# A diffusion step on one core: the weight sums for the way down spread evenly, and the last half product divided at column 320

## The chip, the cores and the metric

The kernel runs on one core of a Trainium2 chip, as one launch. The metric is the device time of an execution in microseconds (us), a median over runs. Five engines work side by side: TensorE (PE, matmuls, with PEld its weight loads), VectorE (DVE), ScalarE (ACT), GpSimd (POOL), and SyncE (SP), which issues nearly all DMA transfers. Each engine takes its instructions strictly in the order of its own queue; a waiting instruction holds what stands behind it.

## The reference

The model is one layer of a diffusion backbone: a half-step FFN, a token mixer (attention and a recurrent scan), a second half-step FFN, and a last RMSNorm. The change lies in the second FFN and the last norm:

```python
x = x + 0.5 * m[8] * swiglu(modulate(x, norm_g[2], m[6], m[7]), *ffn2)   # end of the layer
def swiglu(h, w1, w3, w2):
    return (jax.nn.silu(h @ w1) * (h @ w3)) @ w2
def rmsnorm(x, g):
    xf = x.astype(jnp.float32)
    xf = xf * lax.rsqrt(jnp.mean(xf * xf, axis=-1, keepdims=True) + EPS)
    return (xf * g.astype(jnp.float32)).astype(x.dtype)
```

x has 1152 tokens (1024 latent and 128 context) and D = 1024 features; w1 and w3 are 1024 x 2816, w2 is 2816 x 1024, all in float32. Modulation and gates differ between latent and context tokens.

## The kernel before, in words

**Layout.** Features lie on the 128 partitions, tokens along the free axis: T = 1152 columns, HALF = 576, quarters of QW = 288. The hidden features make NF = 22 blocks `f` of 128. A float32 product is made of three matmuls on parts in the reduced type fp32r: high by high, high by low, low by high. So each matrix needs a high part (a cast on ACT) and a low part (a subtraction on DVE).

**The way up, `ffn_fast(1, ...)`.** Blocks 0 to 2 are plain (`plain_block`). Blocks 3 to 21 are done by a Strassen-Winograd scheme: `fast_block` runs seven products, in the order `PRODUCTS = (1, 6, 7, 5, 2, 4, 3)`, in place of eight. For each product two blocks of tokens (r = 0, 1) take 12 matmuls each of 128 x 288 (L1865), so 24 matmuls are one product, and 19 x 7 = 133 products follow one another. Evictions on ACT and DVE (L1867 to L1883) turn the sums into SiLU(...) times (...), and SP stores the result to `hs` in DRAM (L1757).

The weights of each product are made by the generator `fast_ops`: SP loads two halves of `raw` for each f (L1818, two buffers), POOL adds and subtracts quarters of the weight matrix in pieces of 256 columns (L1836), ACT casts the high part (L1840), DVE subtracts it for the low part (L1841). The list `made` holds the weights of six products ahead of the one in work; their tiles are six buffers under two tags.

**The weight sums for the way down, `combos(w2)`.** The way down also uses seven products instead of eight, so it needs sums of quarters of w2. `combos` makes them in 22 sets (11 blocks `kk` by two halves `v` of the columns). For one set SP loads four pieces of 128 x 256 (L591), POOL makes four additions (L594, L595, L597, L598), and SP stores four results to `wc` in DRAM (L601). The pieces lie in three buffers of one tag and one of another, so a set's loads need the buffers that the last set's stores set free. The generator is advanced once a product (`next(wsum, None)`); a set has five `yield`s, so 22 sets are 110 steps.

**What sets the order.** A scheduler orders the instructions on each engine by costs and due times, not simply in the order in which the program was written, unless an instruction goes through `keep_in_program_order`; that ties it behind the instruction written before it on its engine, without a semaphore. The sums do not go through it before the change.

**The way down, `way_down`.** Six products of the scheme are swept in 66 steps (six products of HF = 11 steps each, 8 cells x 3 matmuls of 128 x 288 per step, L731). SP loads the hidden features `h` (L618) and weights `raw` (L636), DVE and ACT prepare the parts. `gated` adds a finished sum to x (L578). The generator is already advanced from the second product of the last f on, so its first loads stand beside the last products of the way up.

**The last half product and the end.** The last product concerns only half of the tokens (columns 0 to HALF) and four of the eight feature blocks. It is divided at column CUT: first `b0`, columns 0 to CUT, with the first HEAD = 7 of the 11 steps taken step by step over four banks (m = 0 to 3), then the remaining four for one m after the other; then `b1`, columns CUT to HALF, m by m. Its right-hand sides come from `prep3(j)` (L672 cast, L673 subtraction) and its weights from `cast_w3`. Beside it stands the RMSNorm: `square` and the sums over m on POOL (L694, L818), `root` (a matmul by ones called `nps`, L702, then ACT L406 and L407 and DVE L408 to L410), and `finish`, which scales x (DVE L499; ACT L496 and POOL L497 for some m) and issues the stores of the output (L500). The right half of the tokens, `root(HALF, T)` and `finish(HALF, T)`, is dealt with inside `b0`; `root(0, CUT)` is called in the middle of the first m of `b1`, after 18 of its 33 matmuls; `root(CUT, HALF)` and the last `finish` close the program.

Of the kernel before, what the change touches and what calls it, by code (L numbers as in the profile page):

```python
# [9 lines left out]
F32 = mybir.dt.float32  # L10
# [10 lines left out]
P = 128  # L21
# [26 lines left out]
HALF = 2 * QW  # L48
HF = NF // 2
SWEEP = (2, 1, 6, 7, 4, 5)  # L50
STEPS = len(SWEEP) * HF
CELLS = (0, 0, "st"), (1, 0, "up"), (2, 0, "up"), (0, 1, "ps1"), (1, 1, "dn"), (2, 1, "dn"), (3, 0, "up"), (3, 1, "dn")
CUT = 384
HEAD = 7


# [41 lines left out]
class Trunk:  # L98
# [480 lines left out]

    def combos(self, w2):  # L580

        nc = self.nc
        self.wc = self.dp.tile([4, HF, P, HALF - 64], F32, name="wc")
        n = 256
        for kk in range(HF):
            for v in range(2):
                lo, hi = slice(v * n, v * n + n), slice(512 + v * n, 512 + v * n + n)
                t = [self.fp.tile([P, QW], F32, tag="hf", bufs=3, name="wc")[:, :n] for _ in range(3)]
                a11, a21, a22, a12 = t + [self.slim("wc")[:, :n]]
                for o, f, c in ((a22, kk + HF, hi), (a21, kk, hi), (a11, kk, lo), (a12, kk + HF, lo)):  # L590
                    nc.sync.dma_start(o, w2[f][:, 0, c])  # L591
                yield
                yield
                nc.gpsimd.tensor_add(a22, a22, a21)  # L594
                nc.gpsimd.tensor_sub(a21, a11, a21)  # L595
                yield
                nc.gpsimd.tensor_sub(a11, a22, a11)  # L597
                nc.gpsimd.tensor_sub(a12, a12, a11)  # L598
                yield
                for i, o in enumerate((a22, a21, a11, a12)):  # L600
                    nc.sync.dma_start(self.wc[i, kk][:, lo], o)  # L601
                yield

    def way_down(self, w2, gm):

        nc = self.nc
# [7 lines left out]
        def load(g, j, h):  # L614
            if kt[g][j] is None:
                new = partial(self.tt, F32) if not g or j < 3 else self.wide
                kt[g][j] = new(name=f"h{g}")
            nc.sync.dma_start(kt[g][j][:, half[h]], self.hs[g * HF + j][:, half[h]])  # L618

        def load_x(m, cs):  # L620
            if self.x[m] is None:
                self.x[m] = self.tt(F32, f"x{m}")
            nc.sync.dma_start(self.x[m][:, cs], self.xs[m][:, cs])
# [9 lines left out]
        def load_w(p):  # L633
            t = raws[p] = self.wp.tile([P, 2, 512], F32, tag="raw", bufs=2, name="raw")
            for v in range(2):
                nc.sync.dma_start(t[:, v], src(2 * p + v))  # L636

        def cast_w(p):
            t = raws.pop(p)
            wh = self.wp.tile([P, 2, 512], F32R, tag="wh", bufs=3, name="wh")  # L640
            wl = self.wp.tile([P, 2, 512], F32R, tag="wl", bufs=3, name="wl")
            nc.scalar.copy(wh, t)  # L642
            nc.vector.tensor_sub(wl, t, wh)  # L643
            for v in range(2):
                W[2 * p + v] = wh[:, v], wl[:, v]

        def first(j):
            t = kt[0][j]
            nc.vector.tensor_sub(t[:, B], t[:, B], t[:, A])  # L649

        def second(j):
            t = kt[1][j]
            nc.vector.tensor_sub(t[:, B], t[:, B], kt[0][j][:, B])  # L653

        def prep(s):
            i, j = SWEEP[s // HF], s % HF
            h0, h1 = kt[0][j], kt[1][j]
            if i == 7:
                nc.vector.tensor_sub(h0[:, A], h1[:, B], h0[:, A])
            elif i == 4:  # L660
                nc.vector.tensor_sub(h1[:, A], h1[:, A], h1[:, B])
            v = {2: (h1, A), 1: (h0, A), 6: (h1, B), 7: (h0, A), 4: (h1, A), 5: (h0, B)}[i]
            v = v[0][:, v[1]]
            hi, lo = self.half("xh", F32R), self.half("xl", F32R)
            nc.scalar.copy(hi, v)
            nc.vector.tensor_sub(lo, v, hi)  # L666
            X[s] = hi, lo

        def prep3(j):
            t = kt[1][j]  # L670
            hi, lo = F(t[:, A]), F(t[:, B])
            nc.scalar.copy(hi, t[:, B])  # L672
            nc.vector.tensor_sub(lo, t[:, B], hi)  # L673

        def load_w3(j):
            t = self.tt(F32, "w3")
            nc.sync.dma_start(t[:, 512:1024], self.wc[3, j])
            w3.append(t)

        def cast_w3(j):  # L680
            t = w3[j]
            nc.scalar.copy(F(t[:, :512]), t[:, 512:1024])
            nc.vector.tensor_sub(F(t[:, 512:1024]), t[:, 512:1024], F(t[:, :512]))

        def square(m, lo, hi):
            acc = self.rs[:, lo:hi]
            if m == (0 if lo else 4):
                nc.scalar.activation(acc, self.x[m][:, lo:hi], AF.Square)
                return
            for c in range(lo, hi, QW):  # L690
                sq = self.slim("sq")
                n = min(QW, hi - c)
                nc.scalar.activation(sq[:, :n], self.x[m][:, c : c + n], AF.Square)
                nc.gpsimd.tensor_add(self.rs[:, c : c + n], self.rs[:, c : c + n], sq[:, :n])  # L694
# [40 lines left out]
        def taken(i, m, r):  # L735
            a, b = HALF + r * QW, r * QW
            outs = {2: ((0, a),), 1: ((0, a),), 6: ((0, b),), 7: ((4, b),), 4: ((4, a),), 5: ((4, b), (0, b))}
            for o, lo in outs[i]:
                self.gated(m + o, banks[m, r], lo, lo + QW, gm)

        for s in range(STEPS):
            i, kk = SWEEP[s // HF], s % HF
            if s % 2 == 0 and s // 2 + 1 < STEPS // 2:
                cast_w(s // 2 + 1)
                if s // 2 + 2 < STEPS // 2:
                    load_w(s // 2 + 2)
            if s + 6 < HF:
                load(1, s + 6, "a")
            if s in (1, 3, 5, 7):
                load_x(s // 2, A)  # L750
            for g, h, at in ((0, "a", 4), (0, "b", 9), (1, "b", 14), (1, "b", 44)):
                if at <= s < at + HF:
                    if at == 44:
                        kt[1][s - at] = None
                    load(g, s - at, h)
            if 25 <= s < 29:
                load_x(s - 25, B)
            if s in (30, 32, 34, 36):
                load_x(s // 2 - 11, slice(0, T))
            if 14 <= s < 14 + HF:  # L760
                first(s - 14)
            if 20 <= s < 20 + HF:
                second(s - 20)
            if s == 45:
                self.lnexp()
            if s == 50:
                self.new_rs()
            if 52 <= s < 52 + HF:
                load_w3(s - 52)
            if 54 <= s < 54 + HF:  # L770
                cast_w3(s - 54)
            if s + 2 < STEPS:
                prep(s + 2)
            if s > 56 and s % 2:
                prep3((s - 57) // 2)
            if 57 <= s < 57 + KT:
                square(s - 57, HALF, T)
            if kk == 0 and i in (2, 1, 5):
                banks = {(m, r): self.bank(tag, "down") for m, r, tag in CELLS}
            if s == STEPS - 2:  # L780
                continue
            both = s == STEPS - 1
            cells = sorted(CELLS, key=lambda c: c[1]) if both else CELLS
            for m, r, _ in cells:
                if both:
                    mms(s - 1, m, r, False, False)
                mms(s, m, r, kk == 0 and i not in (6, 7, 4), kk == HF - 1)
                if kk == HF - 1:
                    taken(i, m, r)

        b0 = [self.bank(t, "down", CUT) for t in ("st", "up", "up", "up")]

# [3 lines left out]
            self.mm3(ps, [(wh, wl, xh, xl)], start=j == 0, stop=j == HF - 1)  # L796

        for j in range(HEAD):
            if j + 5 < HF:
                prep3(j + 5)  # L800
            for m in range(4):
                mm(b0[m], m, j, 0, CUT)
            if j == 2:
                for r in range(2):
                    root(HALF + r * QW, HALF + (r + 1) * QW, ("dn", "ps1")[r])
            if j == 3:
                self.finish(HALF, T)
            if j > 2:
                square(j + 1, 0, HALF)
        b1 = [self.bank(t, "down", HALF - CUT) for t in ("dn", "dn", "dn", "ps1")]  # L810
        for m in range(4):
            for j in range(HEAD, HF):
                mm(b0[m], m, j, 0, CUT)
            self.gated(m, b0[m], 0, CUT, gm)
            sq = self.half("sq")[:, :CUT]
            nc.scalar.activation(sq, self.x[m][:, :CUT], AF.Square)
# [1305 lines left out]
```

## Time and profile before

| what | number |
|---|---|
| median of 3 runs | 2995.68 us (2993.05 to 2998.06) |
| profiled execution | 2989.97 us, its span 2988.2 us |
| mean granted clock of TensorE | 0.981 |
| stage of the fast blocks, second FFN | about 2248 to 2724 us of the span |
| the sums (first load to last store) | about 2172 to 2446 us |
| the sweep of the way down | to 2937.6 us |
| the last half product and the end | 2937.6 to 2988.2 us |

The profiled execution is 5.7 us below the median, so a sum is made against the execution's own 2989.97 us. A row of a window gives the stretch, then busy time and number of instructions for each engine asked for, the granted clock (1.00 is full), the share of the DMA engines and what they moved. A row of groups gives line, engine, operation, tiles and shapes, then busy time and mean duration in ns, then the idle time ahead of it and what ended it. A row of waits gives who waited for whom, the total, how often, and the longest.

### The profile page before, as it was taken

The page shows a single profiled execution, that of the slowest core. Times are in us where ns is not written, and L with a number is a line of the kernel's source. Part 1 is how long each engine was busy: PE and PEld are TensorE (multiplying, and loading weights), DVE is VectorE, ACT ScalarE, POOL GpSimd, SP SyncE. Part 2 cuts the span into 40 slices and gives each one's busy share as a digit, 9 for nine tenths or more (in the row PEclk, how much of TensorE's full clock was granted, in tenths as well). Part 3 has the DMA queues.
Part 4 walks back from the last instruction along what each step waited for, and adds up shares of the span by engine and source line. Part 5 has one row for each costly group of instructions (what it writes and reads, how often), then busy time and mean ns, then how long its engine had stood idle before and what let it go on. Part 6 is the DMA issues. An engine that isn't in the chain of part 4 may idle for free. (4 is left out here: it accounts for less than half of the span.)

```text
span 2988.2 us, 57736 instructions
## 1 busy us (share of the span) xinstructions
PE 2852.0 (95%) x22928; PEld 2711.9 (91%) x22928; DVE 1903.2 (64%) x3655; ACT 1179.4 (39%) x2218; POOL 1040.3 (35%) x967
## 2 busy tenths in 40 slices
PE   7999999999989999999998999899999789999998
PEld 5999999999988989898996777699999779999998
DVE  7787777566657657575247776856664445556865
ACT  5432322221273435342236777721542222323453
POOL 3233323553143333332244444533345542220003
PEclk9999999999999999999998999999999889999999
DMA  6643343632111111111201111342445652227442
GB/s 236 203 144 122 121 128 111 227 115 68 54 61 62 39 54 39 55 39 59 77 13 36 41 32 59 100 158 82 163 156 163 197 165 73 75 76 262 154 140 78
DMA packets 187214, 316.61 MB, mean 106 GB/s; under 512 B 23168, under 2 KB 110272, under 8 KB 186944
## 3 DMA queue, kind: packets, MB, share of 16 engines
q1 hardware_dynamic: 186800, 312.83, 32.0%
q8 instruction: 180, 2.95, 0.4%
q14 instruction: 90, 0.74, 0.1%
q10 hardware_dynamic: 144, 0.10, 0.0%
HBM read 237.79 MB, written 75.06 MB: 105 GB/s over the span
## 5 line engine op out<-in xcount | busy, mean ns | idle before, releaser
L1865 PE MATMUL b<-xo,wo 128*128 128x288 f32 x3552 | 491.0, 298 | 17.6 <-DVE et L1871 17.6
L1865 PEld LDWEIGHTS b<-xo,wo 128*128 128x128 f32 x3552 | 481.6, 190 | 18.6 <-DVE et L1871 18.6
L1865 PE MATMUL b<-bh,wo 128*128 128x288 f32 x1776 | 372.4, 299 | 20.1 <-ACT et L1875 20.1
L506 PE MATMUL mm<-xh,wh 128*128 128x384 f32 (+1 forms) x1008 | 354.2, 351 | 26.4 <-DVE sg L939 13.8
L508 PE MATMUL mm<-xh,wl 128*128 128x384 f32 (+1 forms) x1008 | 343.5, 341 | 0.8 <-DVE wl L246 0.8
L507 PE MATMUL mm<-xl,wh 128*128 128x384 f32 (+1 forms) x1008 | 343.2, 340 | 0.7 <-issue 0.7
L246 POOL TENSOR_TENSOR wl<-raw,wh 128x1024 fp32r<-128x1024 f32 (+1 forms) x92 | 206.3, 2244 | 369.6 <-ACT wh L245 338.5
L1865 PEld LDWEIGHTS b<-bh,wo 128*128 128x128 f32 x1776 | 294.9, 192 | 20.9 <-ACT et L1875 20.9
L535 DVE SCALAR_TENSOR_TENSOR x<-dn,modt,x 128x384 f32<-128x384 f32 (+4 forms) x440 | 211.3, 499 | 119.6 <-PE dn L508 118.7
L1865 PE MATMUL b<-bl,wo 128*128 128x288 f32 x888 | 264.9, 298 | 0.0
L506 PEld LDWEIGHTS mm<-xh,wh 128*128 128x128 f32 (+1 forms) x1008 | 190.8, 189 | 35.5 <-DVE sg L939 15.5
L1841 DVE TENSOR_TENSOR wo<-raw,wo 128x512 fp32r<-128x512 f32 x185 | 129.8, 703 | 132.9 <-ACT wo L1840 130.9
L1840 ACT CAST wo<-raw 128x512 fp32r<-128x512 f32 x185 | 114.1, 621 | 232.7 <-PE b L1865 100.3
L507 PEld LDWEIGHTS mm<-xl,wh 128*128 128x128 f32 (+1 forms) x1008 | 191.2, 190 | 3.5 <-issue 2.2
L508 PEld LDWEIGHTS mm<-xh,wl 128*128 128x128 f32 (+1 forms) x1008 | 191.0, 189 | 2.1 <-DVE wl L246 1.1
L1597 POOL TENSOR_TENSOR ehl<-e,ehl 128x512 fp32r<-128x512 f32 x93 | 122.9, 1322 | 144.8 <-ACT ehl L1595 65.1
L1865 PEld LDWEIGHTS b<-bl,wo 128*128 128x128 f32 x888 | 170.8, 192 | 0.0
L245 ACT CAST wh<-raw 128x1024 fp32r<-128x1024 f32 (+3 forms) x97 | 92.8, 959 | 163.8 <-PE mm L507 61.5
L731 PE MATMUL down<-xh,wh 128*128 128x288 f32 x528 | 156.4, 297 | 0.5 <-DVE x L578 0.5
L731 PE MATMUL down<-xl,wh 128*128 128x288 f32 x528 | 155.9, 296 | 0.8 <-DVE xl L666 0.8
L731 PE MATMUL down<-xh,wl 128*128 128x288 f32 x528 | 156.1, 296 | 0.0
L1836 POOL TENSOR_TENSOR ws<-raw 128x256 f32<-128x256 f32 x74 | 67.7, 934 | 250.7 <-DMA raw<-in_w 227.2
(419 smaller groups left out, 7284.7 us busy)
## 6 DMA issues: line engine op xcount, KB each, us to landing
raw<-in_w SPq DMA_DIRECT2D x181, 256.0 KB, 3.1
hs<-et SPq DMA_DIRECT2D x148, 144.0 KB, 1.8
raw<-in_w_in SPq DMA_DIRECT2D x41, 512.0 KB, 3.7
wada<-in_w_aT SPq DMA_DIRECT2D x80, 256.0 KB, 2.9
raw<-in_w SPq DMA_DIRECT2D x36, 512.0 KB, 3.7
wada<-in_w_ada SPq DMA_DIRECT2D x32, 512.0 KB, 4.0
h<-hs SPq DMA_DIRECT2D x55, 288.0 KB, 5.1
hb<-hd SPq DMA_DIRECT2D x44, 288.0 KB, 3.6
```

The costliest lines, as they stand in the source:

```text
L245: pin(self.nc.scalar.copy(wh, raw))
L246: pin((eng or self.nc.gpsimd).tensor_sub(wl, raw, wh))
L506: nc.tensor.matmul(ps, wh, xh, start=start and i == 0, stop=False)
L507: nc.tensor.matmul(ps, wh, xl, start=False, stop=False)
L508: nc.tensor.matmul(ps, wl, xh, start=False, stop=stop and i == n - 1)
L535: nc.vector.scalar_tensor_tensor(self.x[m][:, a:b], ps[:, a - lo : b - lo], self.modt[:, gm, m, s : s + 1], self.x[m][:, a:b], ALU.mult, A ...
L731: nc.tensor.matmul(banks[m, r], w, x, start=first and i == 0, stop=last and i == 2, skip_group_check=chain)
L1597: eng.tensor_sub(el, e, eh)
L1836: nc.gpsimd.tensor_tensor(o[:, c], x[:, c], y[:, c], op)
L1840: nc.scalar.copy(wh, src[i])
L1841: nc.vector.tensor_sub(wl, src[i], wh)
L1865: nc.tensor.matmul(ps, w[:, k], x[:, k, :QW], start=first, stop=last, skip_group_check=home != i)
```

## The change

It has three parts. First, `combos`: a set now has six `yield`s (a step between the last additions and the stores), so 22 sets are 132 steps, and each load, addition and store goes through `keep_in_program_order`. (The DRAM tile is written as 512 columns where HALF - 64 stood, which is the same number.) Second, CUT becomes 320: the left part of the last half product is 320 columns wide instead of 384, the right part 256 instead of 192; and inside the left part `root(HALF, T)` and `finish(HALF, T)` are called after six steps (j == 5) instead of after three and four, and the squares of x for m = 4 to 7 at j = 0 to 3 instead of 3 to 6. Third, `prep3` is called at steps 48 to 63 of the sweep, in the fifth and sixth product, instead of at odd steps from 57 on and in the first steps of the left part.

```diff
-CUT = 384
+CUT = 320
...
-        nc = self.nc
-        self.wc = self.dp.tile([4, HF, P, HALF - 64], F32, name="wc")
+        nc, pin = self.nc, self.tc.keep_in_program_order
+        self.wc = self.dp.tile([4, HF, P, 512], F32, name="wc")
...
                 for o, f, c in ((a22, kk + HF, hi), (a21, kk, hi), (a11, kk, lo), (a12, kk + HF, lo)):
-                    nc.sync.dma_start(o, w2[f][:, 0, c])
+                    pin(nc.sync.dma_start(o, w2[f][:, 0, c]))
                 yield
                 yield
-                nc.gpsimd.tensor_add(a22, a22, a21)
-                nc.gpsimd.tensor_sub(a21, a11, a21)
+                pin(nc.gpsimd.tensor_add(a22, a22, a21))
+                pin(nc.gpsimd.tensor_sub(a21, a11, a21))
                 yield
-                nc.gpsimd.tensor_sub(a11, a22, a11)
-                nc.gpsimd.tensor_sub(a12, a12, a11)
+                pin(nc.gpsimd.tensor_sub(a11, a22, a11))
+                pin(nc.gpsimd.tensor_sub(a12, a12, a11))
+                yield
                 yield
                 for i, o in enumerate((a22, a21, a11, a12)):
-                    nc.sync.dma_start(self.wc[i, kk][:, lo], o)
+                    pin(nc.sync.dma_start(self.wc[i, kk][:, lo], o))
                 yield
...
+        third = [48 + (3 * j + 1) // 2 for j in range(HF)]
...
-            if s > 56 and s % 2:
-                prep3((s - 57) // 2)
+            if s in third:
+                prep3(third.index(s))
...
         for j in range(HEAD):
-            if j + 5 < HF:
-                prep3(j + 5)
             for m in range(4):
                 mm(b0[m], m, j, 0, CUT)
-            if j == 2:
+            if j == 5:
                 for r in range(2):
                     root(HALF + r * QW, HALF + (r + 1) * QW, ("dn", "ps1")[r])
-            if j == 3:
                 self.finish(HALF, T)
-            if j > 2:
-                square(j + 1, 0, HALF)
+            if j < 4:
+                square(j + 4, 0, HALF)
```

What this does to the order of the instructions is best seen at three places. Line numbers of the changed kernel are one higher between its lines 602 and 741, and one lower behind its line 831; L1835 there is L1836 before, L602 is L601.

The first place is POOL in the middle of the fast blocks. L1836 makes the pre-additions of the products' weights (`ws`, `raw`); the other rows are additions of sets. Before:

```order
L1836 TENSOR_TENSOR raw<-raw,ws 128x256 x2
L594 TENSOR_TENSOR wc<-wc 128x256
L595 TENSOR_TENSOR wc<-wc 128x256
L597 TENSOR_TENSOR wc<-wc 128x256
L598 TENSOR_TENSOR wc<-wc 128x256
L594 TENSOR_TENSOR wc<-wc 128x256
L595 TENSOR_TENSOR wc<-wc 128x256
L597 TENSOR_TENSOR wc<-wc 128x256
L598 TENSOR_TENSOR wc<-wc 128x256
L1836 TENSOR_TENSOR ws<-raw 128x256 x2
```

And now:

```order
L1835 TENSOR_TENSOR raw<-raw,ws 128x256 x2
L1835 TENSOR_TENSOR ws<-raw 128x256 x2
L1835 TENSOR_TENSOR ws<-ws,raw 128x256 x2
L1835 TENSOR_TENSOR raw<-raw 128x256 x2
L594 TENSOR_TENSOR wc<-wc 128x256
L595 TENSOR_TENSOR wc<-wc 128x256
L597 TENSOR_TENSOR wc<-wc 128x256
L598 TENSOR_TENSOR wc<-wc 128x256
L1835 TENSOR_TENSOR raw<-raw,ws 128x256 x2
```

Two whole sets stood in a gap between pre-additions, up to four in one f, and behind the middle of the stage none were left. Now about one set stands in each f, up to the last.

The second place is SP at the change from the way up to the way down. `hs` are stores of the way up, `h` and `raw` of L636/L637 loads of the way down. Before:

```order
L1818 DMA raw<-in_w 128x512 x2
L636 DMA raw<-in_w 128x512 x2
L1757 DMA hs_23744<-et 128x288 x4
L618 DMA h_29454<-hs_23744 128x576
L618 DMA h_29456<-hs_23744 128x576
L618 DMA h_29489<-hs_23744 128x576
L636 DMA raw<-in_w 128x512 x2
L618 DMA h_29538<-hs_23744 128x576
```

And now:

```order
L637 DMA raw<-in_w 128x512 x2
L1756 DMA hs_23744<-et 128x288 x2
L602 DMA wc<-wc 128x256 x4
L1756 DMA hs_23744<-et 128x288 x2
L591 DMA wc<-in_w 128x256 x4
L619 DMA h_29446<-hs_23744 128x576
L619 DMA h_29448<-hs_23744 128x576
L619 DMA h_29483<-hs_23744 128x576
L637 DMA raw<-in_w 128x512 x2
L619 DMA h_29534<-hs_23744 128x576
L619 DMA h_29562<-hs_23744 128x576
L602 DMA wc<-wc 128x256 x4
```

The last set's loads and stores (`wc`) now stand among the first loads of the way down, where none stood.

The third place is DVE in the last half product: L578 adds a finished sum to x, L408 to L410 are the end of a `root`, L499 belongs to `finish`. Before, from the last L499 over the right half of the tokens on:

```order
L499 SCALAR_TENSOR_TENSOR x_30924<-x_30924,vec,rs 128x576
L578 SCALAR_TENSOR_TENSOR x_29683<-down,modt,x_29683 128x384
L578 SCALAR_TENSOR_TENSOR x_29752<-down,modt,x_29752 128x384
L578 SCALAR_TENSOR_TENSOR x_29821<-down,modt,x_29821 128x384
L578 SCALAR_TENSOR_TENSOR x_29890<-down,modt,x_29890 128x384
L408 SCALAR_TENSOR_TENSOR rt<-nps,rs 128x384
L409 SCALAR_TENSOR_TENSOR rt<-rt,rs 128x384
L410 SCALAR_TENSOR_TENSOR rs<-rt,rs 128x384
```

And now:

```order
L499 SCALAR_TENSOR_TENSOR x_30924<-x_30924,vec,rs 128x576
L578 SCALAR_TENSOR_TENSOR x_29683<-down,modt,x_29683 128x320
L578 SCALAR_TENSOR_TENSOR x_29752<-down,modt,x_29752 128x320
L578 SCALAR_TENSOR_TENSOR x_29821<-down,modt,x_29821 128x320
L578 SCALAR_TENSOR_TENSOR x_29890<-down,modt,x_29890 128x320
L408 SCALAR_TENSOR_TENSOR rt<-nps,rs 128x320
L409 SCALAR_TENSOR_TENSOR rt<-rt,rs 128x320
L578 SCALAR_TENSOR_TENSOR x_29683<-down,modt,x_29683 128x256
```

The six L499 over the right half still stand ahead of the four evictions of the left part, though their `root` is now called three steps later on PE; the widths change, and the first eviction of the right part moves ahead of the last root operation.

## The prediction

> **What bounds the kernel now.** I read the page first, for the share of each engine and the chain of waits.
>
> ```profile
> span 2988.2 us, 57736 instructions
> PE 2852.0 (95%) x22928; PEld 2711.9 (91%) x22928; DVE 1903.2 (64%) x3655; ACT 1179.4 (39%) x2218; POOL 1040.3 (35%) x967
> PE b L1865 9%; PE down L731 6%; PE down L508 0%; PE down L507 0%; PE down L506 0%; DMA h<-hs 0%; DVE wl L643 0%; POOL rs L694 0%; PE nps L702 0%; DVE xl L666 0%; DVE h L649 0%; DMA raw<-in_w 0%; ACT wh L642 0%; DVE x L499 0%; DVE h L653 0%
> ```
>
> TensorE (PE) is busy for 95%, and the chain runs over two matmul lines: L1865, the products of the fast blocks, and L731, the way down. A saving must close a gap in PE, make a matmul cheaper, or shorten what follows the last one. So the next view is windows over L1865 alone: three stretches of the second FFN, and the same code in the first FFN, which makes no weight sums.
>
> ```profile
> core 0: us, PE busy (x) PEld busy (x), PEclk, DMA share, GB/s
> 2248.60:2288.60 40.00, 39.97 (x300) 39.80 (x300) 1.00 0.51 161
> 2288.60:2450.70 162.10, 125.64 (x854) 124.28 (x853) 0.89 0.58 186
> 2450.70:2724.00 273.30, 273.27 (x2040) 273.03 (x2040) 0.99 0.28 93
> 154.00:557.00 403.00, 401.71 (x3023) 401.52 (x3024) 1.00 0.40 129
> ```
>
> In the first FFN 3024 matmuls take 403 us, 133.3 ns each. In the second FFN 40 us run at that pace, then 162.1 us hold 854 matmuls, which at 133.3 ns need 113.8 us, and the last 273 us are full again. The loss of the stage is 162.1 - 113.8 = **48.3 us**, all in one stretch. The waits of PE from 2240 to 2724 us and two rows of its timeline say what it consists of.
>
> ```profile
> PE b L1865 <- ACT et L1875: 18.8, 3, 7.6
> PE b L1865 <- DVE et L1871: 17.6, 4, 6.3
> 2352.96 3.15 PE L1865 MATMUL b<-xo,wo 128*128 128x288 f32 x12 [3.63 <-DVE et L1871]
> 2438.09 4.99 PE L1865 MATMUL b<-xo,wo 128*128 128x288 f32 x24 [2.50 <-DVE et L1871]
> ```
>
> Seven stalls make 36.4 us. The other 12 us are slow matmuls behind them: 12 take 3.15 us where the pace gives 1.6, and 24 take 4.99 instead of 3.2. The named releasers (L1871, L1875) are the last evictions ahead; they cannot be the cause, since the first FFN runs them too. All waits of the same stretch show the cause:
>
> ```profile
> ACT wo L1840 <- POOL ws L1836: 78.7, 6, 16.4
> POOL wc L594 <- DMA wc<-in_w: 39.7, 11, 5.0
> ACT wo L1840 <- POOL raw L1836: 30.7, 10, 10.2
> SPq L601 <- POOL wc L594: 35.9, 16, 5.7
> ```
>
> The cast L1840, which makes the next weights, waits 109 us for GpSimd's (POOL's) pre-additions L1836, and POOL stands 39.7 us at L594 for the loads of a set of weight sums. Its order explains it: two whole sets stand in one gap between pre-additions, and the second set's loads need buffers that the first set's stores must free, so POOL waits in order with the products' additions behind it.
>
> **The change part by part. Sums spread out.** The POOL groups of this stretch, and the last two rows the stretch after it, in which no sums are left:
>
> ```profile
> L595 POOL TENSOR_TENSOR wc<-wc 128x256 f32<-128x256 f32 x17 | 15.5, 913 | 3.3 <-issue 1.5 <-POOL wc L594 0.4 <-DMA wc<-in_w 0.2
> L597 POOL TENSOR_TENSOR wc<-wc 128x256 f32<-128x256 f32 x17 | 15.2, 891 | 1.3
> L598 POOL TENSOR_TENSOR wc<-wc 128x256 f32<-128x256 f32 x17 | 14.2, 836 | 1.3
> L594 POOL TENSOR_TENSOR wc<-wc 128x256 f32<-128x256 f32 x17 | 14.0, 826 | 52.3 <-DMA wc<-in_w 39.7 <-DMA raw<-in_w 5.9 <-DMA hs<-et 3.9
> L1836 POOL TENSOR_TENSOR ws<-raw 128x256 f32<-128x256 f32 x22 | 17.9, 832 | 83.7 <-DMA raw<-in_w 83.7
> L1836 POOL TENSOR_TENSOR raw<-raw,ws 128x256 f32<-128x256 f32 x24 | 17.4, 745 | 102.0 <-issue 102.0
> ```
>
> No addition and no transfer is removed. A set costs POOL 0.83+0.91+0.89+0.84 = 3.5 us, and up to 5.0 us at L594 if its loads are late: 8.5 us at most. Before, a gap held two sets, so 17, and the longest wait of a cast was 16.4. Now 22 sets take 132 of the 133 products, one set in six products, 19 to 20 us of PE time (6 x 24 x 133.3 ns = 19.2). Against that stands the lead: weights are made six products, 19.2 us, ahead. From it go the path of a product's weights:
>
> ```profile
> raw<-in_w SPq DMA_DIRECT2D x181, 256.0 KB, 3.1
> L1840 ACT CAST wo<-raw 128x512 fp32r<-128x512 f32 x185 | 114.1, 621 | 232.7 <-PE b L1865 100.3
> L1841 DVE TENSOR_TENSOR wo<-raw,wo 128x512 fp32r<-128x512 f32 x185 | 129.8, 703 | 132.9 <-ACT wo L1840 130.9
> ```
>
> 3.1 for the load, 4 x 0.75 for pre-additions, 0.6 for the cast, 0.7 for the low part: 7.4 us. About 11.8 us of slack remain, and one set with its full wait is 8.5. So no stall is due, and the whole 48.3 goes. Room on POOL: without sums it idles 83.7 + 102.0 us in 273, some 15 us in each 22.4 us of an f (168 matmuls x 133.3 ns); 1.16 sets per f take 4. Each set's stores stand two products behind its last additions, so SP, which waited 35.9 us at L601, should find them ready. The margin is thin (11.8 against 8.5), and a set's waits may add to a late raw load: I leave **+2 us** of stalls, between 0 and 12 (a stall of 2.5 with its 1.8 of slow matmuls, three times). The start of the sums moves too: nothing stands in the plain blocks any longer. At the rows above nothing is lost there, so 0, between -1.5 and +1 by the few stalls ahead of 2248 us.
>
> **The sums now end at the door of the way down.** Before, they ended at 2446 us; now the last set's loads and stores stand on SP among the first loads of h and raw. These windows show the room (PE, PEld, DVE, ACT, POOL, then clock, DMA share, GB/s):
>
> ```profile
> 2690.00:2708.00 18.00, 18.00 (x138) 18.00 (x138) 9.71 (x17) 6.50 (x13) 2.65 (x4) 1.00 0.33 109
> 2708.00:2762.00 54.00, 53.48 (x400) 52.98 (x398) 35.65 (x57) 18.21 (x26) 0.00 (x0) 1.00 0.92 312
> 2762.00:2790.00 28.00, 28.00 (x211) 27.88 (x210) 27.44 (x40) 12.01 (x17) 0.00 (x0) 1.00 0.84 301
> ```
>
> The DMA engines are 92% busy there, yet PE loses 0.52 us in 54. One set is 4 x 128 KB in and as much out, 1 MB, which at 312 GB/s takes 3.4 us; whatever of it delays a load that PE then waits for is lost. Between 0 and 4, I take **+1.5**.
>
> **Low parts earlier.** prep3 is issued from step 48 on instead of 57. Its rows stand at nearly the same places of ACT's and DVE's order as before, since the scheduler had already drawn them forward: **0**, hidden beside full PE steps. Should all eleven fall into DVE's full stretches, one cast and one subtraction (0.6 + 0.7) each could be late once: +1.3 at most.
>
> **Column 320.** Paces of PE by width, from windows of the line that forms `down`: 288, 384 and 192 columns.
>
> ```profile
> 2859.72:2904.00 44.28, 44.28 (x335) 44.28 (x334) 7.66 (x20) 1.00 0.53 155
> 2937.64:2943.95 6.31, 6.31 (x38) 6.15 (x36) 1.50 (x4) 1.00 0.00 1
> 2964.73:2977.73 13.00, 13.00 (x114) 12.86 (x114) 1.14 (x3) 1.00 0.33 122
> ```
>
> 133 ns, 175 ns (6.31/36) and 114 ns (13.00/114). 320 lies between 133 and 175: 147 by a straight line. 256 lies between 114 and 133. The slope of the two wide rows, 42 ns for 96 columns, carried down gives 119 for 256 and 91 for 192; 114 was measured for 192, so a floor holds there, and 256 stands just above it: I take 120 (the straight line from 192 to 288 would give 127). 132 matmuls of each: before 132 x (0.175 + 0.114) = 38.2 us, now 132 x (0.147 + 0.120) = 35.2, a gain of 3 us, or 2 at 127. But the order around it changes as well. Rows of the tail, where root(HALF, T) (`nps`) starts a chain that ends in six DVE operations:
>
> ```profile
> 2943.95 1.13 PE L702 MATMUL nps<-rs,ones 128*128 128x288 f32 x4
> 2948.23 6.91 DVE L499 SCALAR_TENSOR_TENSOR x<-x,vec,rs 128x576 f32<-128x576 f32 x6
> 2955.59 0.62 DVE L578 SCALAR_TENSOR_TENSOR x<-down,modt,x 128x384 f32<-128x384 f32 x1 [0.45 <-PE down L508]
> 2956.91 1.01 POOL L818 TENSOR_TENSOR rs<-rs,sq 128x384 f32<-128x384 f32 x1 [5.30 <-ACT sq L816]
> 2962.58 0.52 ACT L816 ACTIVATE sq<-x 128x384 f32<-128x384 f32 x1 [1.59 <-DVE x L578]
> 2963.71 0.83 PE L702 MATMUL nps<-rs,ones 128*128 128x384 f32 x2
> 2977.93 0.42 DVE L578 SCALAR_TENSOR_TENSOR x<-down,modt,x 128x192 f32<-128x192 f32 x1 [2.52 <-PE down L508]
> 2981.45 2.73 DVE L499 SCALAR_TENSOR_TENSOR x<-x,vec,rs 128x192 f32<-128x192 f32 x6
> ```
>
> I count from T0 = 2937.64, the first 384-wide product. Before, `nps` stood at 6.3, the six L499 ended at 17.5 (2955.14), and the first eviction of the left part followed at 17.95. Now root stands after six groups instead of three: 6 x 12 x 0.147 = 10.6, and with the same 11.2 us of chain DVE is free at 21.8. PE is through the left part at 132 x 0.147 + 1.0 = 20.4, and after 18 products of the right part, at 22.6, it wants root(0, CUT). That needs the four evictions (21.8 to 23.9), the squares (0.5) and three POOL additions of some 0.85 in a row: ready at about 25.5. **PE stalls for 3 us**, which it did not before. By the 2.50 us stall above 1.8 us of slow matmuls follow. Then 0.4 for the root and 114 x 0.120 = 13.7: the last product ends at 25.5 + 0.4 + 1.8 + 13.7 = 41.4, against 40.1 before (2977.73). Behind it stand ten and a half us to the end, of which the eviction, the square, the three root operations and the last six L499 grow from 192 to 256 columns. The L499 rows give 0.46 us for 192 and 1.15 for 576, so 0.58 for 256: 0.12 x 6 at most, and 0.06 each for five others, 1.0. Sum of the tail: 1.3 + 1.0 = **+2.3**, between -2 (no stall) and +5 (stall and slow clock both longer).
>
> [...]
>
> **Sum.** -48.3 + 2 + 1.5 + 0 + 2.3 = -42.5. The profiled execution spans 2988.2 us with 1.8 outside, 2990.0; it lies 5.7 below the median of the runs, 2995.7. So the profile should say about 2947.5, the median about 2953; I say 2952.5.
>
> **The rivals.**
> (a) *Half of the stalls stay.* For it: 11.8 against 8.5 us of margin, and POOL's order puts each set ahead of the next product's additions. Against it: the longest cast wait, 16.4, fits two sets. Half of 48.3 is kept, so -24 + 3.8 = -20: 2975. Chance 0.17.
> (b) *Full gain and a tail without the stall*: -48.3 + 1.5 - 2 = -49, so 2947. For it: the chain of root, or the squares, may run faster than the rows that I add. Against it: the six L499 hold DVE in order ahead of the evictions. Chance 0.14.
> (c) *Slower.* SP is one queue: if a set's stores wait on POOL, the raw loads of the next f wait behind them. It decides once the raw load is more than the 11.8 us late; then every f stalls anew, say 2.6 us with 1.6 of slow matmuls, 19 x 4.2 = 80, so -43 + 80 = +37: 3032. The longest wait at L601 was 5.7 us with two sets in a gap, which speaks against it. Chance 0.04.
> (d) *The pins do nothing*, the scheduler draws sets forward as before: within 6 us, 2996. POOL's order as built shows one set per gap to the end. Chance 0.03.
>
> **How the numbers follow.** My forecast has 0.62. About 0.2%, 6 us, is what a measurement of this kernel can tell from no change. Faster: 0.62 + 0.17 + 0.14 = 0.93, same 0.03, slower 0.04. All low bounds together, -48.3 + 0 + 0 - 2 - 1.5 = -52, give 2944; all high ones, -48.3 + 12 + 4 + 1.3 + 5 + 1 = -25, give 2971. To hold the middle of rival (a) as well, the range is **2942 to 2975**.
>
> **What would show it.** In the profile after: L1865 without idle time from 2250 us to the way down and PEclk near 1.00; casts L1840 waiting for POOL only in the order of us; sets at even spacing, 22 us for 1.16 of them, up to the last product; a wait of PE at `nps` of the narrower root of about 3 us with slow matmuls behind it. Wrong would be a stall at L1865 after L594 waits, PE waiting for h or xl in the first 50 us of the way down, or a tail from the first left product to the end shorter than the 50.6 us of now (2988.2 - 2937.64).

## The result, and the profile after

The changed kernel takes 2946.45 us (median of 4 runs, 2941.23 to 2951.87) against 2995.17 for the kernel before: a ratio of 0.9837, 95% interval 0.9815 to 0.9859, or 48.7 us less. Foretold were 2952.5, between 2942 and 2975. Its profiled execution spans 2947.4 us.

The page of the changed kernel:

```profile
span 2947.4 us, 57739 instructions
PE 2842.7 (96%) x22928; PEld 2703.6 (92%) x22928; DVE 1907.5 (65%) x3655; ACT 1180.8 (40%) x2218; POOL 1043.7 (35%) x967
```

The work is the same to a few instructions; PE is busy for 9 us less: 15 us less in the fast blocks, where the matmuls at the slow clock have gone, 1 less in the tail, and 7 more ahead of the fast blocks. The same windows as before, over the matmuls of the fast blocks (now L1864): stretch, PE busy, PEld busy, granted clock, DMA share, GB/s.

```profile
2255.70:2295.70 40.00, 39.99 (x302) 40.00 (x303) 1.00 0.48 153
2295.70:2450.70 155.00, 155.00 (x1170) 155.00 (x1169) 1.00 0.47 151
2450.70:2679.60 228.90, 228.90 (x1725) 228.78 (x1724) 1.00 0.44 143
```

The stretch with 0.89 of the clock and 36 us of idle time has become full, 1170 matmuls in 155 us. The transfers, which came at 186 GB/s and then at 93, are now level. POOL's groups over the fast blocks show the sets among the pre-additions (L1835 was L1836):

```profile
L1835 POOL TENSOR_TENSOR ws<-raw 128x256 f32<-128x256 f32 x36 | 31.6, 896 | 106.2 <-DMA raw<-in_w 106.2
L594 POOL TENSOR_TENSOR wc<-wc 128x256 f32<-128x256 f32 x21 | 18.0, 856 | 26.9 <-DMA wc<-in_w 26.9
```

POOL now waits for the next f's raw weights, as it did before mainly where no sets were left; for the sets' loads it waits 26.9 us over 424 us, not 39.7 us over 162. Two other waits of the fast blocks, for the experiments below: the cast for POOL, and VectorE's L359, a sum for the gate of this FFN, for its weights `wada`:

```profile
ACT wo L1839 <- POOL ws L1835: 76.2, 17, 6.2
DVE junk L359 <- DMA wada<-in_w_aT: 1.6, 3, 0.6
```

The cast still waits often, but 6.2 us at the longest where it was 16.4, and PE does not stand for it. All waits of PE behind the fast blocks:

```profile
PE nps L703 <- POOL rs L817: 3.1, 1, 3.1
PE down L732 <- DVE x L578: 1.6, 1, 1.6
PE down L732 <- DVE xl L667: 0.8, 1, 0.8
```

The first is new: it is the narrower root of the last half product. Its rows, and those around it:

```profile
2904.65 1.13 PE L703 MATMUL nps<-rs,ones 128*128 128x288 f32 x4
2909.00 6.92 DVE L499 SCALAR_TENSOR_TENSOR x<-x,vec,rs 128x576 f32<-128x576 f32 x6
2915.85 1.91 DVE L578 SCALAR_TENSOR_TENSOR x<-down,modt,x 128x320 f32<-128x320 f32 x4
2917.04 2.73 POOL L817 TENSOR_TENSOR rs<-rs,sq 128x320 f32<-128x320 f32 x3 [4.65 <-ACT sq L815]
2919.82 0.81 PE L703 MATMUL nps<-rs,ones 128*128 128x320 f32 x2 [3.10 <-POOL rs L817]
2921.72 0.41 PE L507 MATMUL down<-h,w 128*128 128x256 f32 x1
2924.00 0.28 PE L506 MATMUL down<-h,w 128*128 128x256 f32 x1
2940.29 3.40 DVE L499 SCALAR_TENSOR_TENSOR x<-x,vec,rs 128x256 f32<-128x256 f32 x6
```

Six L499 hold DVE until 2915.9; then come the evictions, the squares, three additions on POOL, and PE, which has stood 3.10 us. Behind it a matmul takes 0.41 us where 0.28 is the full pace.

Four marks divide each profiled execution: the first fast-block matmul of the second FFN, the first matmul of the way down, the last of its sweep, and the end.

| kernel | to the first | fast blocks | sweep | left part to the end | span |
|---|---|---|---|---|---|
| before | 2248.6 | 475.2 | 213.7 | 50.7 | 2988.2 |
| changed | 2255.7 | 423.9 | 214.4 | 53.4 | 2947.4 |
| difference | +7.1 | -51.3 | +0.7 | +2.7 | -40.8 |

The first column belongs to no edit: the changed kernel run again (as_changed, below) has 2249.0 there.

### The profile page after: what moved, and what is told of

It is laid out like the page before. It is cut to its first block, busy times and chain, and to the rows that moved or that the text cites. A ratio compares the mean times of both kernels' runs of the same rounds, so it can differ in the third digit from the quotient of the medians.

```text
span 2947.4 us, 57739 instructions
## 1 busy us (share of the span) xinstructions
PE 2842.7 (96%) x22928; PEld 2703.6 (92%) x22928; DVE 1907.5 (65%) x3655; ACT 1180.8 (40%) x2218; POOL 1043.7 (35%) x967
## 5 line engine op out<-in xcount | busy, mean ns | idle before, releaser
L1864 PE MATMUL b<-xo,wo 128*128 128x288 f32 x3552 | 484.5, 296 | 0.0
L1864 PEld LDWEIGHTS b<-xo,wo 128*128 128x128 f32 x3552 | 476.3, 188 | 0.0
L1864 PE MATMUL b<-bh,wo 128*128 128x288 f32 x1776 | 365.4, 295 | 1.1 <-ACT et L1874 1.1
L1864 PEld LDWEIGHTS b<-bh,wo 128*128 128x128 f32 x1776 | 288.7, 188 | 1.4 <-ACT et L1874 1.3
L1864 PE MATMUL b<-bl,wo 128*128 128x288 f32 x888 | 261.4, 294 | 0.0
L1864 PEld LDWEIGHTS b<-bl,wo 128*128 128x128 f32 x888 | 167.2, 188 | 0.0
L1835 POOL TENSOR_TENSOR ws<-raw 128x256 f32<-128x256 f32 x74 | 70.8, 976 | 259.2 <-DMA raw<-in_w 233.2
```

Source lines behind the costliest of these rows:

```text
L1835: nc.gpsimd.tensor_tensor(o[:, c], x[:, c], y[:, c], op)
L1864: nc.tensor.matmul(ps, w[:, k], x[:, k, :QW], start=first, stop=last, skip_group_check=home != i)
```

## The experiments

The theory: the whole gain comes from spacing the sets, because POOL takes its work in order (before, L594 stood 39.7 us for loads, with pre-additions behind it); the tail's edits cost 2.7 us through the moved root. The rivals: the tail carries part of the gain; the pins, or the sixth step, matter by themselves; SP's queue and not POOL's is where the weights were late.

**The sums alone, the tail alone, and the changed kernel again.** `sums_only` is the kernel before with the new `combos`; `tail_only` is the rest of the change:

```diff
 sums_only:  the diff of combos as above; CUT = 384 and way_down as before
 tail_only:  combos as before; CUT = 320, root, finish, squares and prep3 as changed
```

> The kernel before with the new weight sums alone (six steps to a set, pinned); the last half product, prep3 and column 384 stay as before. My theory: the whole gain is here. From the first fast-block matmul to the first one of the way down about 424 us (475.2 before), no wait of PE at L1865 over 1 us; from the first 384-wide matmul of the left part to the end 50.6 us as before. So about 3 us less than the changed kernel, 51 less than before. Rival (the tail's edits carry part of the gain): slower than the changed kernel by as much as they give, 1 to 3 us.

> The kernel before with column 320, the moved root, finish and squares, and the earlier prep3; the sums as before. My theory: fast blocks 475 us with the seven stalls as before; from the first matmul of the left part to the end 53.3 us (50.6 before), with a wait of PE of about 3 us at the narrower root: +2.7, not to be told from no change by the time. Rival (PE's 3 us of cheaper matmuls come through): 47.6 to 49 us from the left part to the end.

> The changed kernel itself once more, beside the three others. Fast blocks 424 us, 214.5 us of sweep, 53.3 us from the left part to the end; the way to the first fast-block matmul shows how far that stretch, which the change does not touch, varies (2248.6 us before, 2255.7 in the profile of the changed kernel): within 8 us either way.

| kernel | to the first | fast blocks | sweep | left part to the end | ratio to before, 95% |
|---|---|---|---|---|---|
| sums_only | 2253.5 | 423.8 | 215.3 | 50.7 | 0.9831 (0.9818 to 0.9845) |
| tail_only | 2250.2 | 475.2 | 213.9 | 53.3 | 1.0006 (0.9997 to 1.0015) |
| as_changed | 2249.0 | 423.8 | 213.7 | 54.7 | 0.9842 (0.9828 to 0.9855) |

All the gain is in the sums, and the tail's edits cost 2.6 to 4 us by the trace, which the timing of tail_only cannot tell from nothing. In tail_only the wait came back without the sums:

```profile
PE nps L702 <- POOL rs L816: 3.0, 1, 3.0
```

**The root back at its place.** The changed kernel with this:

```diff
-            if j == 5:
+            if j == 2:
                 for r in range(2):
                     root(HALF + r * QW, HALF + (r + 1) * QW, ("dn", "ps1")[r])
+            if j == 3:
                 self.finish(HALF, T)
-            if j < 4:
-                square(j + 4, 0, HALF)
+            if j > 2:
+                square(j + 1, 0, HALF)
```

> The changed kernel with root and finish of the right half called after three and four steps again, and the squares of m = 4 to 7 at j = 3 to 6, as before; column 320 and the sums stay changed. My theory: the six L499 end 5.3 us earlier, the first eviction of the left part then waits for PE and not PE for it, the 3.1 us at the narrower root and the 1.4 us of slow matmuls behind it go: 48.8 us from the left part to the end (53.3 in the changed kernel), some 4.5 us less than the changed kernel. Rival (the stall comes from the three additions on POOL, whenever they start): still 2 us or more of wait at that root, 51 us or more.

48.5 us from the left part to the end, and no wait at any `nps`: the evictions of the left part go out as PE delivers them (DVE, m = 0 and 1 together, then 2; 3 follows in the same way):

```profile
2898.59 6.91 DVE L499 SCALAR_TENSOR_TENSOR x<-x,vec,rs 128x576 f32<-128x576 f32 x6
2905.42 1.10 DVE L578 SCALAR_TENSOR_TENSOR x<-down,modt,x 128x320 f32<-128x320 f32 x2
2907.72 0.55 DVE L578 SCALAR_TENSOR_TENSOR x<-down,modt,x 128x320 f32<-128x320 f32 x1 [1.21 <-PE down L508]
```

The median is 2938.96 us, ratio 0.9809 (0.9796 to 0.9823), the lowest of all kernels here: below the changed kernel, whose interval in the same runs begins at 0.9828, while the interval of sums_only (from 0.9818) still overlaps. Of the 8.9 us between the medians of as_changed and root_early the tail shows 4.9 to 6.2. So by the trace column 320, with prep3 earlier, is worth 2.2 us (50.7 to 48.5), and the moved root, with the squares, takes 4.9 to 6.2 back.

To see whether the wait follows the root's place, it was called one step earlier than changed (`j == 4`):

> The changed kernel with root and finish of the right half called at j == 4 instead of 5. My theory: DVE is free one group, 12 x 0.147 = 1.76 us, earlier, so the wait of PE at the narrower root falls from 3.1 to about 1.3 us; slow matmuls behind it 0 to 1.4 us; 50.2 to 51.6 us from the left part to the end (53.4 and 54.7 with j == 5, 48.5 with j == 2). Rival (the wait does not follow the root's place): 3 us.

50.1 us, a tenth below the range, and the wait fell by 1.7 us, one group of twelve:

```profile
2916.18 0.81 PE L703 MATMUL nps<-rs,ones 128*128 128x320 f32 x2 [1.37 <-POOL rs L817]
2917.48 0.27 PE L507 MATMUL down<-h,w 128*128 128x256 f32 x1
```

**prep3 at its old steps**, everything else changed:

```diff
-            if s in third:
-                prep3(third.index(s))
+            if s > 56 and s % 2:
+                prep3((s - 57) // 2)
...
+            if j + 5 < HF:
+                prep3(j + 5)
```

> The changed kernel with prep3 at its old steps. My theory: the scheduler had drawn it forward, nothing changes: sweep 213.7 to 215.3 us, 53.4 to 54.7 from the left part to the end. Rival (the earlier low parts keep the left part fed): new waits of PE at `down`, 55 us or more.

Sweep 214.0, left part to the end 54.7, the same 3.1 us at the root: no effect.

**Pins, steps and spacing.** Four forms of `combos` on the kernel before. `six_loose` has the sixth yield and no pins; the others are pinned with five, three and two yields to a set (three: one yield between loads and first additions, none behind the stores; two: all four additions together):

```diff
 pinned_two:
                     pin(nc.sync.dma_start(o, w2[f][:, 0, c]))
                 yield
-                yield
                 pin(nc.gpsimd.tensor_add(a22, a22, a21))
                 pin(nc.gpsimd.tensor_sub(a21, a11, a21))
-                yield
                 pin(nc.gpsimd.tensor_sub(a11, a22, a11))
                 pin(nc.gpsimd.tensor_sub(a12, a12, a11))
                 yield
                 for i, o in enumerate((a22, a21, a11, a12)):
                     pin(nc.sync.dma_start(self.wc[i, kk][:, lo], o))
-                yield
```

> The kernel before with the sixth step to a set, but nothing pinned. My theory: the scheduler draws the sets forward all the same, two to a gap of POOL's pre-additions; fast blocks 465 to 480 us with stalls at L1865, as before (475.2). Rival (the sixth step alone spreads them): 424 us.

> The kernel before with the sums pinned, five steps to a set as before. My theory: one set in 16 us against a slack of 11.8 us still leaves each set alone in its gap, no stall; fast blocks 424 to 428 us, and the last set ends ahead of the way down. Rival (the margin that the sixth step gives is needed): 3 us or more of waits at L1865.

> The kernel before with the sums pinned and three steps to a set: one set in 9.6 us, 2.33 to an f, over 66 products. My theory: POOL's own work is 6 + 2.33 x 3.5 = 14 us in 22.4 and the loads' waits 2 to 5 us a set come on top: 19 to 26 us, the edge. Some stalls, 0 to 20 us lost in all: 424 to 445 us. Rival (pinning alone removes the loss, whatever the spacing): 424 us. Rival (any two sets in one gap cost the full stall): 460 us or more.

> The kernel before with the sums pinned and two steps to a set: loads, then all four additions one product later, then the stores; 3.5 sets to an f, over 44 products, close to the density before. My theory: POOL needs 6 + 3.5 x 3.5 = 18 us in 22.4 and waits 3.5 times for loads that wait for stores, 3 to 5 us each: 29 to 36 us an f, 6.3 f: 40 to 75 us lost, fast blocks 465 to 500 us, although every instruction is pinned. Rival (the pins are what matters): 424 to 430 us.

| kernel | products to a set | fast blocks | lost against 423.8 | one run, before beside it |
|---|---|---|---|---|
| six_loose | as scheduled | 475.4 | 51.6 | 2993.9, 3000.5 |
| pinned_two | 2 | 468.1 | 44.3 | 2984.4, 3000.5 |
| pinned_three | 3 | 438.7 | 14.9 | 2956.8, 3000.5 |
| pinned_five | 5 | 423.8 | 0 | 2944.6, 3000.5 |
| sums_only | 6 | 423.8 | 0 | above |

The loss follows the spacing. Pins without spacing keep most of it (pinned_two), the sixth step without pins keeps all (six_loose), and with pins the sixth step is not needed. The pins only make the written spacing come true. The waits of pinned_two up to 2420 us have the pattern of before (L593 there is the first addition of a set, L1833 the pre-additions, L1837 the cast):

```profile
ACT wo L1837 <- POOL ws L1833: 63.1, 6, 13.5
POOL wc L593 <- DMA wc<-in_w: 37.6, 12, 5.4
```

**POOL or SP.** One stall of the kernel before, step by step: rows of POOL's timeline, and the cast's, around the stall of PE of 6.32 us that ends at 2324.80.

```profile
2311.37 0.73 POOL L594 TENSOR_TENSOR wc<-wc 128x256 f32<-128x256 f32 x1 [3.92 <-DMA hs<-et]
2318.66 0.72 POOL L594 TENSOR_TENSOR wc<-wc 128x256 f32<-128x256 f32 x1 [3.77 <-DMA wc<-in_w]
2321.74 1.40 POOL L1836 TENSOR_TENSOR ws<-raw 128x256 f32<-128x256 f32 x2
2324.99 0.62 ACT L1840 CAST wo<-ws 128x512 fp32r<-128x512 f32 x1 [16.36 <-POOL ws L1836]
```

Two sets take POOL from 2307.5 to 2321.7, over half of it in waits, and the cast stands 16.36 us. But PE goes on at 2324.80, before that cast begins. What it waited for was an eviction on DVE, and DVE's rows show why that was late:

```profile
2323.11 1.26 DVE L359 SCALAR_TENSOR_TENSOR junk<-wada,cb 128x512 bf16<-128x512 f32 x1 [10.45 <-DMA wada<-in_w_aT]
2324.30 0.45 DVE L1871 TENSOR_TENSOR et<-b,et 128x288 f32<-128x288 f32 x1
2324.80 3.25 PE L1865 MATMUL b<-xo,wo 128*128 128x288 f32 x12 [6.32 <-DVE et L1871]
```

DVE stood 10.45 us for a load of `wada`, with the eviction L1871 behind it in its order. SP's rows of the same time show that load, and the raw load of this f, issued late, behind the second set's loads:

```profile
2315.80 1.86 SPq L591 DMA_DIRECT2D wc<-in_w  x4
2317.71 0.90 SPq L1818 DMA_DIRECT2D raw<-in_w  x2
2318.65 0.43 SPq L340 DMA_DIRECT2D wada<-in_w_aT  x1
2319.41 2.72 SPq L601 DMA_DIRECT2D wc<-wc  x4
```

With the 3.1 us that such loads took from issue to landing (median in the profile before) the raw load, issued from 2317.71 on, would be there at about 2321 too, by estimate. The other stalls, followed back in the same way, are of two kinds. Three of the seven (5.20, 6.32 and 3.63 us, 15.2 in all) ended with L1871 right behind an L359 that had waited for `wada`. The other four (6.59, 4.64, 2.50 and 7.58 us, 21.3 in all) ended with an eviction that stood on ACT or DVE behind a cast or low part held up by POOL, as here (PE's row, then ACT's):

```profile
2385.26 0.58 PE L1865 MATMUL b<-bh,wo 128*128 128x288 f32 x1 [6.59 <-ACT et L1875]
2382.86 0.62 ACT L1840 CAST wo<-ws 128x512 fp32r<-128x512 f32 x1 [11.92 <-POOL ws L1836]
2384.75 0.70 ACT L1875 ACTIVATE et<-b 128x288 f32<-128x288 f32 x2
```

So both queues took part: SP's through `wada`, POOL's through the casts. Over the stretch from 2288.6 to 2450.7 us L359 waited 23.3 us, where the changed kernel has 1.6:

```profile
DVE junk L359 <- DMA wada<-in_w_aT: 23.3, 3, 10.4
```

Two kernels try to take the queues apart. The first leaves POOL's part out:

```diff
-                nc.gpsimd.tensor_add(a22, a22, a21)
-                nc.gpsimd.tensor_sub(a21, a11, a21)
...
-                nc.gpsimd.tensor_sub(a11, a22, a11)
-                nc.gpsimd.tensor_sub(a12, a12, a11)
```

> The kernel before without the four additions of a set on POOL: the loads and stores stay, and what is stored is the loaded pieces, so the way down works on wrong weights. My theory (POOL stands in its order before a set's late loads, and the products' pre-additions behind it): no stall at L1865, fast blocks 424 us. Rival (SP's queue: the raw loads stand behind stores and loads of sets that wait on each other): stalls remain, 445 us or more.

438.8 us of fast blocks: neither. The loss fell from 51 to 15 us, but without additions the sets also ran faster, the last stores at 2353 instead of 2446, and SP was packed with them. What is left are waits for raw loads and for `wada`:

```profile
2269.00 2.38 POOL L1832 TENSOR_TENSOR ws<-raw 128x256 f32<-128x256 f32 x2 [13.52 <-DMA raw<-in_w]
2297.34 0.97 DVE L359 SCALAR_TENSOR_TENSOR junk<-wada,cb 128x512 bf16<-128x512 f32 x1 [9.65 <-DMA wada<-in_w_aT]
```

Of the five stalls of PE over 0.8 us (9.6 us) two, 4.2 us, end behind casts whose pre-additions had waited for raw loads, and three, 5.4 us, with L359's waits for `wada`. So SP's queue can hold PE up without the sets' additions on POOL, at a density that the kernel before does not have. The second kernel takes the raw loads off SP and leaves POOL's order:

```diff
-                nc.sync.dma_start(t[:, v], src)
+                nc.scalar.dma_start(t[:, v], src)
```

> The kernel before with the raw loads of the fast blocks (L1818) issued from ACT's queue instead of SP's, so they no longer stand behind the sets' loads and stores; POOL's order keeps two sets to a gap. After the run without additions kept 15 us of the loss, two readings are open. POOL's order: the pre-additions still stand behind two sets that wait for their loads, so the stalls at L1865 stay, fast blocks 455 us or more. SP's queue: the late raw loads were the cause, so most of the 51 us go, 435 us or less. Both in one loop (a set's stores wait for POOL, the next set's loads for the stores, and raw loads and pre-additions stand behind either): the loop through POOL and the set's own loads is left as it was, 450 to 475 us.

473.8 us, nearly the whole loss, with 33 us of waits of PE at L1865. Waits up to 2460 us:

```profile
POOL wc L594 <- DMA wc<-in_w: 63.0, 18, 6.5
ACT wo L1840 <- POOL ws L1836: 41.3, 7, 7.3
ACT wo L1840 <- POOL raw L1836: 29.7, 12, 8.4
POOL ws L1836 <- DMA raw<-in_w: 8.7, 2, 4.6
ACT et L1875 <- DMA wc<-wc: 16.3, 6, 4.0
```

That excludes the reading by which the raw loads' place on SP cost most of the 51 us. The other two, POOL's order alone (455 or more) and both queues in one loop (450 to 475), fit the number alike. Nor is the run a clean one: ACT, which now issues the raw loads, has 33 us of waits that the profile puts down to transfers (16.3 in the last row, three others 17.1) and that the kernel before does not have, and three stalls, 11.3 us, again ended with L359's wait for `wada`. That POOL's order alone would cost the 51 us is therefore not shown. No run moves the loads of `wada`, or the casts' place ahead of the evictions, by itself; what the runs do show is that both kinds of stall go when the sets are spaced.

## Why the prediction was right

**The stage.** The loss was put at 48.3 us and the cause at sets that stand two in a gap. That the sets' density is the cause is shown by the series of spacings. Two terms were mis-sized. The loss is 51.3 by the marks: I measured it in one window, with 133.3 ns for a matmul; all 3192 now run in 423.9 us, 132.8 ns each, and the two windows around the stretch hid the rest. The last of them was taken as full, but began at half the clock, with 20 matmuls in 4.80 us:

```profile
2450.70:2455.50 4.80, 4.80 (x20) 4.80 (x21) 0.50 0.50 170
```

And the +2 us for remaining stalls was 0: there is not one wait at L1864. pinned_five shows that one set in 16 us was enough too, and for three products to a set, where 0 to 20 us were expected, 14.9 came.

**The path from the sets to PE was not as written.** The prediction set the named releasers, the evictions L1871 and L1875, aside, since the first FFN runs them too, and took the stalls for weights that come too late, so that 11.8 us of slack stood against 8.5. But in the kernel before the weights were not late. No product had its low part finished less than 6.3 us ahead of its first matmul (the n-th L1841 beside the n-th group of 24 matmuls); in pinned_three, which lost 14.9 us, the smallest distance was 3.9. The evictions themselves were late, behind waiting instructions in the order of ACT and DVE: casts and low parts that waited for POOL, and L359, which the prediction does not have, waiting for SP. So the slack of 11.8 against 8.5 is not what decided, and that the sum over it came out is luck in this step. The forecast of the stage stands on the density of the sets alone, which governs both paths.

**The door of the way down.** +1.5 was taken, +0.7 came. But the sweep takes 215.0 us in pinned_five, where the last set's store is issued at 2597.4, 80 us ahead of the way down, and 213.7 in as_changed, where sets run to the end. So the +0.7 is no price of the late sets that the runs can show.

**The tail.** +2.3 was taken, +2.7 came, with the mechanism as written: stall foretold 3, found 3.10; narrower root ready 25.5 us after the first product of the left part, found 25.7 (2919.82 - 2894.1); the pace of 320 columns 147 ns, found 146 (below), of 256 columns 120, found 117, 3 ns above the 114 of 192 columns before. Behind the last matmul 0.9 us came for the 1.0: the six L499 alone went from 2.73 to 3.40 us. Paces in the changed kernel:

```profile
2894.10:2904.60 10.50, 10.50 (x74) 10.45 (x72) 1.49 (x4) 1.00 0.01 2
2925.00:2936.00 11.00, 11.00 (x95) 10.99 (x94) 1.00 (x3) 1.00 0.33 119
```

Slow matmuls followed the stall, as taken from the 2.50 us stall of before: the row at 2921.72 above is one, 0.41 us where 0.28 is the full pace, and the clock granted from 2920.49 to 2923.90 us was 0.50 (last section).

**The forecast's own miss** is 6 us, 2952.5 against 2946.5: 3 from the stage's loss, 2 from the stalls that did not come and 0.8 from the sweep, less 0.4 from the tail, make 5.4 of it. What it got right by luck is the reference point. It took the profiled execution of before as 5.7 us below the median and added that back. The stretch ahead of the fast blocks took 2248.6 us in that execution, and between 2249.0 and 2255.7 in the twelve others that are alike up to about 2170 us (all but raw_by_act): the one profiled before was the quickest, the one profiled after the slowest. The sets no longer stand in its last 80 us, but the 7 us are not from there: the last norm ahead of it (`nps`, L478) starts at 2164.1 and at 2171.7. Had the two profiles been compared with each other alone, the gain would have read 40.8 us instead of 48.7.

**The rivals.** Half of the stalls staying, the slower SP queue and ineffective pins all fell. The gain without the stall in the tail was not what this kernel does, but root_early is that case: 48.5 us to the end, where the rival's -2 from 50.6 gave 48.6. That its 2947 for the whole lies nearer to 2946.5 than the forecast is chance: the stall came, and the stage gave 3 us more than either had.

## What to carry to other kernels

An engine that is idle two thirds of the time (POOL here, 35% busy) can still hold up the one that sets the pace (21.3 us of PE's stalls ended with evictions behind casts and low parts that it held up) when its queue holds work that waits for transfers: spread such side work, and hold it there in the order, since a scheduler may draw it together again (six_loose, 475.4 us of fast blocks). And follow a stall back through the order of each engine: here the weights were ready, and what PE lacked were evictions that stood behind a waiting cast, or behind a sum that had nothing to do with the products. When a step is moved later, ask what is queued behind it on every engine: the root moved by three groups was harmless on PE, but the six scalings behind it on VectorE, 6.9 us, stood ahead of the evictions on which the next root depended. And compare executions by stage, between marks, before a difference of a few us is given to an edit.

## What the runs showed of the hardware

A stall of 3.02 to 3.10 us was followed by matmuls 0.21 us apart instead of 0.12 in all four profiles that have it (changed, as_changed, tail_only, prep3_late). One of 2.50 us in the kernel before was followed by slow ones too, 24 in 4.99 us; one of 1.37 us in root_at_four was not. The slow stretch was not equally long each time: 11 matmuls in one profile of the changed kernel, 17 in another (as_changed), with nearly the same stall ahead, 3.10 and 3.07 us, and that is the 1.3 us between 53.4 and 54.7 us for the same code. The stall of the second:

```profile
2912.33 1.44 PE L703 MATMUL nps<-rs,ones 128*128 128x320 f32 x2 [3.07 <-POOL rs L817]
```

The granted clock shows the difference. Windows of PE alone, three of the first profile (stall from 2916.72 to 2919.82), then three of the second (stall from 2909.26 to 2912.33); the clock is the first number behind PE's busy time and matmuls:

```profile
2917.08:2920.49 3.41, 0.67 (x3) 1.00 0.40 157
2920.49:2923.90 3.41, 3.41 (x15) 0.50 0.00 0
2923.90:2936.00 12.10, 12.10 (x104) 1.00 0.31 110
2908.21:2911.62 3.41, 1.05 (x9) 1.00 0.81 312
2911.62:2915.03 3.41, 2.70 (x6) 0.50 0.00 0
2915.03:2918.45 3.42, 3.42 (x18) 0.50 0.02 5
```

In the first profile the clock was 0.50 for 3.41 us, from 0.67 us behind the end of the stall on; in the second for 6.83 us, from 0.71 us ahead of its end on. What sets the beginning and the length is not shown. Nor does half the clock come behind stalls alone: in the kernel before, PE was busy throughout the 6.5 us ahead of one such stretch.

```profile
1326.00:1332.50 6.50, 6.50 (x181) 1.00 0.27 86
1332.53:1335.93 3.40, 3.40 (x13) 0.50 0.00 0
```
